# Long convolution of the latents: the exchange between the inverse block transform and the last transform goes through DRAM

## The chip, the cores and the metric

The kernel runs on one core of a Trainium2 chip, in one launch. The metric is the device time of that core in microseconds (us). The kernel before took 2639.78 us, the median of 3 runs (2636.53 to 2640.61).

## What is computed

One inference step of a hybrid block serves 1024 latent tokens and 256 context tokens of width 1024: a SwiGLU, a mixer and a second SwiGLU, with modulated norms between them. Half of the mixer's channels (512) go through a state-space scan, the other half through two long convolutions in a row. Only the long convolution of the latents is touched:

```python
k2 = jnp.concatenate([k[:, 0], jnp.zeros_like(k[:1, 0]), k[:0:-1, 1]], axis=0)
kf = jnp.fft.rfft(k2, axis=0)
zz = v
for i, gate in enumerate((x1, x2)):
    sf = jnp.fft.rfft(zz, n=2 * l, axis=1)
    conv = jnp.fft.irfft(sf * kf[:, i], n=2 * l, axis=1)[:, :l]
    zz = gate * (conv + zz * skip[i])
```

Here l is 1024, so each convolution is a transform of length 2048 per channel, a product with the filter's spectrum, and the transform back.

## The kernel before, in words

The kernel has stages in time: the filters, the first SwiGLU, the projections with the scan, then the long convolutions (`hyena_lat` for the latents, `hyena_ctx` for the context), the output projection (`wout`) and the second SwiGLU. Everything but the long convolutions and a few small parts stays as it is. In the profile the long convolutions lie between 1448 and 1650 us.

A transform of length 2048 is done as matrix products in two steps, 32 = 16 pairs by 64. The 512 channels are worked on in two halves of 256 (`hf` 0 and 1, called left and right here), and there are two convolutions in a row (`o` 0 and 1). For each `o` and `hf` there are three kinds of items:

- **a**, 4 items: transposes of the signal (`pz`), its split in two parts, the first matrix product (`pa`), and a copy to the tile `uu`.
- **b**, 8 items, each two of the 16 blocks: four transposes of `uu` (`pt`, L1403), a copy (`ut`, L1409), the product with the block's matrix (`pzz`, L1414), the product with the filter's spectrum on VectorE and ScalarE (`yy`, L1419 to L1423), the inverse block transform (`pw`, L1431) and a copy by ScalarE to the tile `vv` (L1435). The spectrum is read from DRAM by four DMAs of 128 KB (`ka` L1394, `kb` L1398) into tiles of a ring with three places, two of which each item takes.
- **c**, 8 items, each a pair `w` of 16 rows: four transposes of `vv` (`pt`, L1457), a copy by ScalarE (`vt`, L1463), and the last transform (`py`, L1469) that sums over all 16 blocks. After each four c items come skip and gate on VectorE (`tm`, L1479, L1482), and for the second convolution a split to `yp`, which the output projection reads.

A c item needs all eight b items of its half, since it reads some of each block: this is the exchange. In `pw` the spectrum tile is the stationary operand, so channels come out as partitions and rows as columns; the transposes of `vv` turn a (row, block) slice back to partitions. All matmuls of `pw`, `pzz` and `py` are float32, and each shows as two instructions in the trace; a transpose shows as one.

What sets the order: `weave` writes one list of items out of three streams (left, right, context), taking at each position the ready item with the lowest rank. An item is ready when the items that it names lie a given number of positions back (b after a: 4, c after b: 8, the next a after c: 4). `pipe` then emits the steps of an item one position apart (`s0` at its own position, the next step at the next). A framework fixes each engine's queue at build time, by this order among what it reckons ready, and adds the waits. Each engine works through its own queue in order. All DMAs are issued by SyncE (SP in the profile). By `weave`, the order of items is: b left of the first convolution alone; c left with b right, one of each in turn; c right with b left of the second convolution; c left with b right of the second convolution; and at the end c right alone. The context's items (`pzr`, `pzi`, `pyc`) and the a items lie between them.

Of the kernel before, what the change touches and what calls it, by code (L numbers as in the profile page):

```python
# [110 lines left out]
class Kern:  # L111
# [1225 lines left out]
    def hyena_lat(self, hc, tp, yh, pp, ptag):  # L1337
# [3 lines left out]
        for q in range(4):  # L1341
            nc.sync.dma_start(z[q], self.hyd[q][:, :LAT])
        cb, cbi, cai = ld("cb", [128, 16, 128]), ld("cbi", [128, 16, 128]), ld("cai", [128, 2, 128])
        ca = [hc.tile([128, 256], F32R, name=f"ca{n}") for n in "hl"]
# [40 lines left out]
        def stage_b(o, hf, b2):  # L1385
            r = {}

            def s0():
                if b2 == 0:
                    st["v", hf] = tp.tile([128, 2, 64, 32], F32, name="vv", tag=f"v{hf}", bufs=1)  # L1390
                r["ka"], r["kb"] = t2("ka", "k", 3), t2("kb", "k", 3)
                k = self.kd[o, b2, :, hf]
# [33 lines left out]
            def s5():  # L1426
                r["pw"] = pst("pw")
                pwv = r["pw"].rearrange("p (q n b s) -> p q n b s", q=2, b=2, s=2)
                for q in range(2):
                    for bb in range(2):  # L1430
                        nc.tensor.matmul(pwv[:, q, :, bb, :], r["y"][:, bb, 128 * q:128 * q + 128],  # L1431
                                         cbi[:, 2 * b2 + bb, :], start=True, stop=True)

            def s6():
                nc.scalar.copy(st["v", hf][:, :, :, 4 * b2:4 * b2 + 4],  # L1435
                               r["pw"].rearrange("p (q n s) -> p q n s", q=2, s=4))
            return [s0, s1, s2, s3, None, None, s5, s6]

        def stage_c(o, hf, v2, v):
# [3 lines left out]
            def s0():  # L1443
                if v == 0:
                    st["py", hf] = [pst("py"), pst("py")]
                if v == 0 and v2 == 0:
                    st["g", hf] = []
                    for q in qs:
                        g = self.raw(f"gate{q}")
                        nc.sync.dma_start(g, self.hyd[4 + 4 * o + q][:, :LAT])  # L1450
                        st["g", hf].append(g)
                r["pys"] = st["py", hf]
                r["pt"] = pst("pt2")
                for ww in range(2):
                    for q in range(2):
                        w = 8 * v2 + 2 * v + ww
                        nc.tensor.transpose(out=r["pt"][:, 256 * ww + 128 * q:256 * ww + 128 * q + 128],  # L1457
                                            in_=st["v", hf][:, q, 4 * w:4 * w + 4, :].rearrange("p n s -> p (n s)"),
                                            identity=self.ident)

            def s1():
                r["vt"] = t2("vt", "ut", 2)
                nc.scalar.copy(r["vt"], pv(r["pt"]))  # L1463

            def s2():
# [6 lines left out]
            def s3():  # L1472
                for q in range(2):
# [9 lines left out]
                    if o:  # L1483
                        for gg in range(2):
                            sg = lambda t: t.rearrange("p (n m) -> p n m", m=64)[:, :, 32 * v2:32 * v2 + 32]
                            self.split(tm[:, 8 * gg:8 * gg + 8, :], *[sg(yh[n][gg][qq][:, 0:512]) for n in range(2)])
            return [s0, s1, s2] + ([s3] if v == 3 else [])

        streams = []
        for hf in range(2):  # L1490
            q = []
            for o in range(2):
                p = o - 1
                need = {"a": [(("c", p, hf, 7), 4)] if o else [], "b": [(("a", o, hf, 3), 4)], "c": [(("b", o, hf, 7), 8)]}
                for kind, its in (("a", [stage_a(o, hf, i2) for i2 in range(4)]),
# [414 lines left out]
def _consts():  # L1910
# [66 lines left out]
    for w in range(2):  # L1977
        for m in range(4):
            for b in range(16):
# [3 lines left out]
                else:  # L1983
                    ai[w, m, b, 0, :, 4 * w + m] = 2 * np.cos(tau * b * r / 32)
                    ai[w, m, b, 1, :, 4 * w + m] = -2 * np.sin(tau * b * r / 32)
    out["cai"] = (ai / 2048).reshape(2, 128, 128).transpose(1, 0, 2)
    tt, f = np.arange(256), np.arange(256)
# [88 lines left out]
```

## Time and profile before

| | us |
|---|---|
| median of 3 runs | 2639.78 |
| the profiled execution, its own time | 2639.89 |
| its span | 2638.1 |
| TensorE (PE) busy in the span | 2552.9 (97%) |
| VectorE (DVE) busy | 1610.3 (61%) |
| ScalarE (ACT) busy | 1061.0 (40%) |
| stretch of the long convolutions, 1448 to 1650 | 202 |
| PE busy in that stretch | 185.18 |
| DVE and ACT busy in that stretch | 123.08 and 142.66 |

The span is the time from the first instruction to the last of one profiled execution. PE is busy nearly all the time over the whole kernel; in the stretch of the long convolutions it is less so. Busy time counts an instruction from its start to its modelled end, and the instructions of PE overlap: the next one starts before the one before has ended.

### The profile page before, as it was taken

What the parts mean: (1) busy time and instruction counts of PE and PEld (TensorE: products, weight loads), DVE (VectorE), ACT (ScalarE), POOL (GpSimd) and SP (SyncE); (2) the same over time, 40 slices, a digit from 0 to 9 for tenths busy, and PEclk for the clock granted to TensorE, in tenths of its full rate; (3) what the DMA queues carried; (4) which work ended last, traced back from release to release, by engine and by line L of the source; (5) the groups of instructions that cost most, each with busy time, mean ns of one, the idle gap of its engine ahead of it and who ended that gap; (6) DMA issues with size and microseconds to landing.
All of it is one profiled execution on the core that took longest, in us unless ns stands there. A gap on an engine that the chain in (4) does not pass through costs nothing.

```text
span 2638.1 us, 39050 instructions
## 1 busy us (share of the span) xinstructions
PE 2552.9 (97%) x15373; PEld 2296.1 (87%) x15373; DVE 1610.3 (61%) x2700; ACT 1061.0 (40%) x1832; POOL 2.4 (0%) x7
## 2 busy tenths in 40 slices
PE   7889999999999999999999899998999999999998
PEld 3559999999988788897778788997999999988888
DVE  7879888865467457507884566578454554443445
ACT  5673222222233335415773686354222222232233
POOL 0000000000000000000000000000000000000000
PEclk9989999999999999999999999998999999999999
DMA  7423444332286446211224453731222222263434
GB/s 262 144 88 103 127 141 132 127 102 73 66 279 216 144 155 197 73 49 57 73 75 164 128 153 115 231 114 49 85 62 69 79 64 67 79 210 117 137 121 152
DMA packets 159180, 321.66 MB, mean 122 GB/s; under 512 B 18055, under 2 KB 62991, under 8 KB 158611
## 3 DMA queue, kind: packets, MB, share of 16 engines
q1 hardware_dynamic: 158995, 319.15, 37.6%
q8 instruction: 121, 1.98, 0.3%
q14 instruction: 64, 0.52, 0.1%
HBM read 250.26 MB, written 68.82 MB: 121 GB/s over the span
## 4 chain that ended last, share of the span: by engine, by line
PE 85%; DVE 6%; ACT 4%; DMA 3%; issue 2%; SPq 0%; DVEq 0%; ACTq 0%
PE pp L653 13%; PE pp L652 13%; PE pp L654 13%; PE pd L653 7%; PE pd L652 7%; PE pd L654 7%; PE pc L652 3%; PE pc L654 3%; PE pc L653 3%; PE po L653 1%; PE po L654 1%; PE po L652 1%; PE pseg L991 1%; DMA wd<-wdn 1%; PE pfa L1239 1%
## 5 line engine op out<-in xcount | busy, mean ns | idle before, releaser
L653 PE MATMUL pd<-hs,dh 128*128 128x512 f32 (+1 forms) x1008 | 358.2, 356 | 0.2
L652 PE MATMUL pd<-hs,dh 128*128 128x512 f32 (+1 forms) x1008 | 355.9, 356 | 2.0 <-DVE nm L226 1.6
L654 PE MATMUL pd<-hs,dl 128*128 128x512 f32 (+1 forms) x1008 | 357.4, 356 | 0.1
L139 DVE TENSOR_TENSOR dl<-wd,dh 128x1024 fp32r<-128x1024 f32 x106 | 129.6, 1224 | 196.0 <-ACT dh L138 190.3
L138 ACT CAST wT<-t 128x512 fp32r<-128x512 f32 x168 | 103.8, 620 | 320.4 <-PE pp L654 234.9
L138 ACT CAST dh<-wd 128x1024 fp32r<-128x1024 f32 x106 | 111.1, 1048 | 298.6 <-PE pd L653 191.7
L652 PEld LDWEIGHTS pd<-hs,dh 128*128 128x128 f32 x1008 | 188.7, 188 | 34.2 <-DVE nm L226 3.8
L652 PE MATMUL pp<-yp,wT 128*128 128x320 f32 x672 | 210.4, 313 | 7.3 <-ACT yp L138 3.8
L653 PEld LDWEIGHTS pd<-hs,dh 128*128 128x128 f32 x1008 | 190.1, 189 | 29.2 <-DVE hs L139 0.6
L654 PEld LDWEIGHTS pd<-hs,dl 128*128 128x128 f32 x1008 | 189.8, 188 | 28.8 <-DVE dl L139 0.5
L652 PE MATMUL pp<-sy,wT 128*128 128x320 f32 x672 | 208.9, 311 | 3.1 <-ACT sy L138 3.1
L654 PE MATMUL pp<-yp,wT 128*128 128x320 f32 x672 | 209.7, 312 | 0.0
L654 PE MATMUL pp<-sy,wT 128*128 128x320 f32 x672 | 208.3, 310 | 0.0
L652 PE MATMUL pp<-sh,wB 128*128 128x320 f32 x672 | 208.0, 309 | 0.0
L654 PE MATMUL pp<-sh,wB 128*128 128x320 f32 x672 | 207.5, 309 | 0.0
L179 DVE CUSTOM_DVE_ANT_0 junk<-wa,scb 128x1024 bf16<-128x1024 f32 x144 | 175.7, 1220 | 41.0 <-DMA wa<-wada 39.9
L139 DVE TENSOR_TENSOR wT<-t,wT 128x512 fp32r<-128x512 f32 x168 | 115.4, 687 | 74.4 <-ACT wT L138 74.0
L138 ACT CAST wB<-wg 128x512 fp32r<-128x512 f32 x126 | 78.0, 621 | 203.4 <-PE pp L654 132.3
L652 PE MATMUL pc<-h,wh 128*128 128x512 f32 (+1 forms) x432 | 156.3, 362 | 0.5 <-DVE xr L615 0.5
L653 PE MATMUL pc<-h,wh 128*128 128x512 f32 (+1 forms) x432 | 154.2, 357 | 0.0
L654 PE MATMUL pc<-h,wl 128*128 128x512 f32 (+1 forms) x432 | 154.1, 357 | 0.0
L652 PEld LDWEIGHTS pp<-yp,wT 128*128 128x128 f32 x672 | 128.2, 191 | 8.2 <-ACT yp L138 4.5
(391 smaller groups left out, 6207.1 us busy)
## 6 DMA issues: line engine op xcount, KB each, us to landing
wd<-wdn SPq DMA_DIRECT2D x100, 512.0 KB, 3.7
wg<-wgu SPq DMA_DIRECT2D x84, 512.0 KB, 3.8
wa<-wada SPq DMA_DIRECT2D x72, 512.0 KB, 3.8
hraw<-hida SPq DMA_DIRECT2D x42, 256.0 KB, 3.6
hraw<-hidd SPq DMA_DIRECT2D x42, 256.0 KB, 3.1
wr<-wc SPq DMA_DIRECT2D x18, 512.0 KB, 3.5
kd<-fk SPq DMA_DIRECT2D x32, 256.0 KB, 2.5
ka<-kd SPq DMA_DIRECT2D x64, 128.0 KB, 2.7
```

Of the source, the lines that this page charges most:

```text
L138: nc.scalar.copy(hi, src)
L139: nc.vector.tensor_tensor(out=lo, in0=src, in1=hi.bitcast(F32), op=ALU.subtract)
L179: nc.vector.tensor_tensor_reduce(out=junk, in0=w, in1=self.scb[cond], scale=1.0, scalar=0.0, op0=ALU.mult, op1=ALU.add, accum_out=self.mod ...
L652: nc.tensor.matmul(ps, wh, rh, start=first, stop=False, **more)
L653: nc.tensor.matmul(ps, wh, rl, start=False, stop=False, **more)
L654: nc.tensor.matmul(ps, wl, rh, start=False, stop=last, **more)
L991: nc.tensor.matmul(q["seg"], self.trir[:, d, :], t, start=d == 0 and n == 0, stop=d == 1 and n == 1)
L1239: nc.tensor.matmul(r["pa"][:, qs], r["k2"][:, qs], caf, start=True, stop=True)
```

## The change

The inverse block transform `pw` gets its operands exchanged: the block's matrix `cbi` is the stationary operand and the product `yy` the moving one, so rows come out as partitions and the 256 channels as columns. Two products of 256 columns take the place of four of 128. ScalarE copies the result to a new tile `vw` (ring of three), and two DMAs per b item write it to a DRAM tile `zv`. A c item reads its pair of rows from `zv` by one DMA straight into `vt` (ring of four), with (block, row) as partitions; its transposes and its ScalarE copy are gone, and the last product `py` stays with a reordered constant. The tile `vv` is gone, the ring of `ka` and `kb` has six places in place of three, and `py` of a c item is emitted three positions after its first step (it was two). The next a items may follow five positions after the last c (it was four).

```diff
@@ stage_b
             def s0():
-                if b2 == 0:
-                    st["v", hf] = tp.tile([128, 2, 64, 32], F32, name="vv", tag=f"v{hf}", bufs=1)
-                r["ka"], r["kb"] = t2("ka", "k", 3), t2("kb", "k", 3)
+                r["ka"], r["kb"] = t2("ka", "k", 6), t2("kb", "k", 6)
...
             def s5():
                 r["pw"] = pst("pw")
-                pwv = r["pw"].rearrange("p (q n b s) -> p q n b s", q=2, b=2, s=2)
-                for q in range(2):
-                    for bb in range(2):
-                        nc.tensor.matmul(pwv[:, q, :, bb, :], r["y"][:, bb, 128 * q:128 * q + 128],
-                                         cbi[:, 2 * b2 + bb, :], start=True, stop=True)
+                for bb in range(2):
+                    nc.tensor.matmul(r["pw"][:, 256 * bb:256 * bb + 256], cbi[:, 2 * b2 + bb, :], r["y"][:, bb, :],
+                                     start=True, stop=True)
 
             def s6():
-                nc.scalar.copy(st["v", hf][:, :, :, 4 * b2:4 * b2 + 4],
-                               r["pw"].rearrange("p (q n s) -> p q n s", q=2, s=4))
+                t = t2("vw", "vw", 3)
+                nc.scalar.copy(t, pv(r["pw"]))
+                for bb in range(2):
+                    nc.sync.dma_start(self.zv[o][hf][:, 2 * b2 + bb], t[:, bb, :])
...
@@ stage_c
-                r["pt"] = pst("pt2")
-                for ww in range(2):
-                    for q in range(2):
-                        w = 8 * v2 + 2 * v + ww
-                        nc.tensor.transpose(out=r["pt"][:, 256 * ww + 128 * q:256 * ww + 128 * q + 128],
-                                            in_=st["v", hf][:, q, 4 * w:4 * w + 4, :].rearrange("p n s -> p (n s)"),
-                                            identity=self.ident)
-
-            def s1():
-                r["vt"] = t2("vt", "ut", 2)
-                nc.scalar.copy(r["vt"], pv(r["pt"]))
-
+                r["vt"] = t2("vt", "vt", 4)
+                w = 8 * v2 + 2 * v
+                nc.sync.dma_start(r["vt"], self.zv[o][hf][w:w + 2].rearrange("w b r c -> (b r) w c"))
...
-            return [s0, s1, s2] + ([s3] if v == 3 else [])
-
+            return [s0, None, None, s2] + ([s3] if v == 3 else [])
+
+        self.zv = [[self.dp.tile([16, 16, 8, 256], F32, name=f"zv{o}{hf}") for hf in range(2)] for o in range(2)]
...
-                need = {"a": [(("c", p, hf, 7), 4)] if o else [], "b": [(("a", o, hf, 3), 4)], "c": [(("b", o, hf, 7), 8)]}
+                need = {"a": [(("c", p, hf, 7), 5)] if o else [], "b": [(("a", o, hf, 3), 4)], "c": [(("b", o, hf, 7), 8)]}
```

The constant `cai` is stored with its 128 rows in the new order (`caih`).

## Rows read from the trace of the kernel before

**Rows 1.** Chain that ended last between 1440 and 1665 us, shares by line.

```profile
by line: PE py L1469 8.4%; PE pw L1431 7.9%; ACT uu L1381 7.0%; PE pzz L1414 5.5%; issue 5.3%; PE pt L1457 4.0%; DVE yy L1422 3.4%; PE pzr L1538 3.3%; DMA yraw<-ysd 3.2%; ACT yy L1421 3.1%; PE pyc L1561 3.1%; PE pzi L1538 3.1%; ACT yy L1420
```

**Rows 2.** Stretches: us; PE, PEld, DVE, ACT, POOL busy (count); clock, DMA share, GB/s.

```profile
1463.60:1503.50 39.90, 35.52 (x203) 28.84 (x202) 25.27 (x39) 27.12 (x42) 0.00 (x0) 0.96 0.48 146
...
1618.00:1634.60 16.60, 13.17 (x72) 11.70 (x70) 13.01 (x29) 8.49 (x21) 0.00 (x0) 0.90 0.54 175
1634.60:1650.00 15.40, 14.31 (x98) 13.85 (x99) 6.71 (x13) 9.52 (x18) 0.00 (x0) 0.77 0.21 69
```

**Rows 3.** TensorE in order of time: one pair of b and c items, 1520 to 1525.

```profile
1521.06 1.06 PE L1469 MATMUL py<-c_cai,vt 128*128 128x128 f32 x8
1521.95 0.60 PE L1457 MATMUL pt<-ident,vv 128*128 128x128 f32 x4
1522.39 1.06 PE L1431 MATMUL pw<-c_cbi,yy 128*128 128x128 f32 x8
1523.29 1.03 PE L1414 MATMUL pzz<-ut,c_cb 128*128 128x256 f32 x4
1524.15 0.60 PE L1403 MATMUL pt<-ident,uu 128*128 128x128 f32 x4
```

**Rows 4.** Groups of instructions, 1446 to 1655: busy us, mean ns, idle before.

```profile
L1457 PE MATMUL pt<-ident,vv 128*128 128x128 f32 x128 | 20.0, 287 | 0.7 <-ACT vv L1435 0.7
...
L1435 ACT COPY vv<-pw 128x512 f32<-128x512 f32 x32 | 18.7, 589 | 8.6 <-PE pw L1431 8.3
```

**Rows 5.** Issues on the spectrum's DRAM tensor: ns min/median/max on the SP queue.

```profile
L1394 SPq DMA_DIRECT2D ka<-kd x64: 444/448/1465, 1451.9 to 1622.9; - x64
L1398 SPq DMA_DIRECT2D kb<-kd x64: 444/588/607, 1453.0 to 1624.6; - x64
L1277 SPq DMA_DIRECT2D kd<-fk x32: 512/513/1010, 92.2 to 185.3; - x32
```

**Rows 6.** DMA issues of 140 to 190 and of 1446 to 1655: us to landing.

```profile
kd<-fk SPq DMA_DIRECT2D x16, 256.0 KB, 2.4
...
gatec<-hyd SPq DMA_DIRECT2D x4, 256.0 KB, 2.8
```

**Rows 7.** The last of `pw` and the first of c: first convolution left, right, second left.

```profile
1497.73 1.05 PE L1431 MATMUL pw<-c_cbi,yy 128*128 128x128 f32 x8
...
1503.51 1.04 PE L1457 MATMUL pt<-ident,vv 128*128 128x128 f32 x8
...
1542.71 1.05 PE L1431 MATMUL pw<-c_cbi,yy 128*128 128x128 f32 x8
...
1545.47 1.04 PE L1457 MATMUL pt<-ident,vv 128*128 128x128 f32 x8
...
1582.14 1.13 PE L1431 MATMUL pw<-c_cbi,yy 128*128 128x128 f32 x8 [1.25 <-DVE yy L1423]
...
1592.83 1.04 PE L1457 MATMUL pt<-ident,vv 128*128 128x128 f32 x8
```

**Rows 8.** What the SP queue waited for, 1400 to 1680: us, times, longest.

```profile
SPq L1398 <- DVE yy L1419: 31.1, 10, 7.4
```

**Rows 9.** Chain of waits, then instructions in time: last b, last c items.

```profile
1622.92 5.08 DMA ka<-kd
...
1632.48 2.05 PE L1431 MATMUL pw<-c_cbi,yy 128*128 128x128 f32 x8 [3.36 <-DVE yy L1423]
1637.05 2.08 PE L1469 MATMUL py<-c_cai,vt 128*128 128x128 f32 x8
1638.92 1.06 PE L1457 MATMUL pt<-ident,vv 128*128 128x128 f32 x4
1648.83 1.16 PE L1469 MATMUL py<-c_cai,vt 128*128 128x128 f32 x8 [0.48 <-ACT vt L1463]
```

**Rows 10.** A stretch of the mixed stage, and SP issues beside other large transfers.

```profile
1552.00:1572.00 20.00, 19.57 (x153) 18.39 (x153) 14.37 (x24) 16.03 (x29) 0.00 (x0) 1.00 0.47 140
...
92.25 3.13 SPq L1277 DMA_DIRECT2D kd<-fk  x3
```

More of the change, by code (lines that the diff above doesn't have):

```diff
@@ L1342, in hyena_lat @@
             nc.sync.dma_start(z[q], self.hyd[q][:, :LAT])
-        cb, cbi, cai = ld("cb", [128, 16, 128]), ld("cbi", [128, 16, 128]), ld("cai", [128, 2, 128])
+        cb, cbi, cai = ld("cb", [128, 16, 128]), ld("cbi", [128, 16, 128]), ld("caih", [128, 2, 128])
         ca = [hc.tile([128, 256], F32R, name=f"ca{n}") for n in "hl"]
@@ L1985, in _consts @@
                     ai[w, m, b, 1, :, 4 * w + m] = -2 * np.sin(tau * b * r / 32)
-    out["cai"] = (ai / 2048).reshape(2, 128, 128).transpose(1, 0, 2)
+    out["caih"] = (ai / 2048).reshape(2, 4, 16, 2, 128).transpose(2, 1, 3, 0, 4).reshape(128, 2, 128)
     tt, f = np.arange(256), np.arange(256)
```

## The prediction

> **What bounds the kernel now.** I began with the page's busy shares and its slices: TensorE is near full all along and thins out only a little between 1448 and 1650 us, where the long convolutions lie. So the question is whether TensorE sets the end in that stretch too. The chain of waits answers it [rows 1]: TensorE's lines lead (`py`, `pw`, `pzz`), but ScalarE's copies, VectorE's `yy` and issue have shares of several per cent, so it is a mixture. The table by stretch splits the mixture [rows 2, 10]. In the mixed stages, where c items of one half alternate with b items of the other, TensorE is busy 19.57 of 20 us: it is the bound there. In 1463.6 to 1503.5, mostly b items alone, it is busy 35.52 of 39.9; at the end, 1618 to 1634.6, 13.17 of 16.6, and the clock falls (0.90, then 0.77).
>
> What TensorE needs for a pair of items is read from starts in order of time [rows 3]: `py` 1521.06 to 1521.95, 0.89; transposes of `vv` 0.44; `pw` 0.90; `pzz` 0.86; transposes of `uu` another 0.44 (the same four instructions). That is 3.53 us per pair.
>
> The Trainium skill ("Trainium Kernel Development and Optimization", Performance Expectations) says matmul busy time is a poor measure because matmuls are pipelined. The row agrees: the 32 groups of `vv` transposes have 20.0 us busy [rows 4], 0.63 each, against 0.44 by their starts. By busy time the first term below would be 24 x 0.63 = 15.1 instead of 10.6, and the forecast 4.5 us lower.
>
> **The change part by part.**
>
> *Transposes of `vv` and their copy.* 24 of the 32 c items lie in three mixed stages that TensorE bounds; each loses 0.44: 24 x 0.44 = 10.6 us gained. The ScalarE copies that go (32, of the form that took 0.589 [rows 4]) gain nothing by themselves, as ScalarE has slack there (16.03 of 20 [rows 10]); bounds 0 to 2 us, I take 0.
>
> *`pw` with exchanged operands.* Four instructions of 256 columns, as `pzz` has: 0.86 for 0.90 [rows 3]. 24 x 0.04 = 1.0 us gained. Its copy has the same shape.
>
> *Three more DMA issues per pair on the SP queue.* Nearest row for both write and read: an issue of 256 KB in 1 KB rows, 0.513 [rows 5]. Loads cost 2 x 0.448 + 2 x 0.588 = 2.07 per b item, so a pair needs 2.07 + 3 x 0.513 = 3.61 us of SP, more than the 3.05 us that TensorE would then need (3.53 - 0.44 - 0.04). What hides it is the ring of six: loads of three items can go out before a mixed stage begins. Inside a stage of eight pairs there are then five loads, about five pairs of writes (a write comes seven positions after its item's load) and eight reads: 5 x 2.07 + 5 x 1.03 + 8 x 0.51 = 19.6 of 24.4 us. I take 0. Without that cover the pair goes at 3.61 and the 11.6 us of the first two terms become a loss of 24 x 0.08 = 1.9. The writes wait for ScalarE's copy; behind them in the queue stand reads and later loads, which are used three positions after their issue at the earliest.
>
> *DMA engines.* Loads alone take a share of 0.47 at 140 GB/s [rows 10], so 298 GB/s would fill them. A stage's loads (5 x 0.524 MB), writes (5 x 0.262) and reads (8 x 0.262) are 6.0 MB or 20.2 us of 24.4: 83%. It fits, with little room; cost 0 to 3 us, I take 0.
>
> *Round trip at the start of c.* The first `py` now waits for copy 0.59 [rows 4], two write issues 1.03 [rows 5], a landing 2.4 and a read's landing 2.8 [rows 6]: 6.8 us after the last `pw`. Before it was copy, transposes, copy: 1.6 without waits. Left, first convolution: last `pw` ends about 1498.6 (start and 0.90), other work runs to 1503.5 [rows 7], cover 4.9, so a gap of 1.9; now it is 0.15, since the eight transposes fill 0.88 of the 1.03 until the first copy is done: +1.75. Right: `pw` ends about 1543.6, cover to 1545.5, a gap of up to 4.9 against 0.15, but b items of the other half are nearly ready and can be put into it: between 0 and 4.75, I take 1.55. Left, second convolution: from 1583.0 to 1592.8 other products run [rows 7], 9.8 of cover: 0. Together +3.3 (0 to 6.5).
>
> *The ring of six, b items alone.* The SP queue waited 31.1 us for `kb` places in ten waits [rows 8]. TensorE's idle time in that stretch is 4.4 us [rows 2]; the gain lies between 0 and that. VectorE's chain through `yy` (three places, unchanged) is late next, so I take 2.
>
> *The ring of six, last b item.* Its `ka` was issued at 1622.92 and took 5.08 to land; `pw` followed at 1632.48 after 3.36 idle, and at a clock that had fallen took 2.05 instead of 1.06 [rows 9, 3]. Loaded three items earlier, the item waits for nothing but its `pzz`, and its VectorE and ScalarE steps lie beside the products that TensorE still has. Gain 0 to 4.4, I take 4.
>
> *The last eight c items alone.* Nothing covers the round trip here. Before: from the copy to the end of `py` about 1634.6 to 1650, 15.4 us [rows 2, 9]. After: 6.8 for the round trip; TensorE idles meanwhile, and after an idle time half as long the clock fell to 1.2 GHz for some us (mean 0.77 [rows 2], `py` 1.87 apart, 1637.05 to 1638.92 [rows 9]). Three `py` at 1.87 and five at 0.89 make 10.1. 16.9 against 15.4: +1.5. Bounds: no fall of the clock and a faster trip, -2; reads that come in two rounds through the ring of four, or stand behind weight loads of the output projection in the SP queue, +6.
>
> Sum: -10.6 - 1.0 + 3.3 - 2 - 4 + 1.5 = -12.8. From the profiled execution's 2639.9 (span 2638.1 and 1.8 around it), which is the median of the runs to 0.1: **2627**.
>
> **Rivals.**
>
> 1. *The SP queue sets the pace, no change.* The loads are not taken ahead in time and a pair takes 3.61. For: 3.61 is well above 3.05, and a load can go out early only if its place is free and nothing that waits stands ahead of it. Against: six places hold the loads of three items. +1.9 + 3.3 - 2 - 4 + 1.5 = +0.7: 2641, or a little below where some loads come early.
>
> 2. *The queue is stopped by its own writes, slower.* A pair of writes at the head of the SP queue waits for ScalarE's copy, and loads behind it are late for VectorE, which makes the next copy late. With one copy's 0.59 per pair: 3.61 + 0.59 = 4.20, 24 x 0.67 = +16.1, with the other terms (-1.2) +14.9: 2655. It is slower by over 0.2% from 3.80 per pair on, a stop of 0.19. For: three issues beside other transfers took 3.13 us [rows 10], so a full DMA system alone can stretch issues that far. Against: loads have three positions of slack.
>
> 3. *Landings are late.* The trip's landings come out near the longest here, 5.08 [rows 9] in place of 2.4 for the writes: 2.7 more at three starts (the fourth is covered), +8: 2635. For: DMA engines at 83%. Against: 2.4 and 2.8 are medians of quiet and of busy stretches. The Trainium skill ("Perfetto Trace Analysis", DMA Instruction — HWDGE) says the write's completion can be surprisingly long when the target is HBM. The rows disagree so far: DRAM writes land in 2.4, reads in 2.8 [rows 6].
>
> That the exchange isn't replaced as described (transposes remain) can be excluded: nothing else transposes in c.
>
> **How the numbers follow.** Forecast 0.54, with its own range 2617 to 2634 (bounds about the sum: the trip +3.2 and -3.3, the two ring terms +6 and -2.8, the end +4.5 and -3.5, not all at once). Rival 1 0.20, rival 2 0.14, rival 3 0.12. 0.2% is 5.3 us, about what a measurement of this kernel can tell from no change. Rival 3 lies at that line and is halved: faster 0.60. Rival 1 and the other half: same 0.25. Slower 0.15. The range for 8 in 10 takes in the forecast, rivals 1 and 3: 2616 to 2645; rival 2 is left out.
>
> **What would show it.** In the mixed stages `py` of neighbouring c items should start 3.05 to 3.2 apart in place of 3.53; 3.6 speaks for rival 1, 3.8 and more, with SP waiting on ScalarE's copy, for rival 2. VectorE should wait no more for `ka` before the last `yy`. Before the last eight `py` TensorE should be idle for about 6 us and its clock lower after it. The landings of `zv` writes and `vt` reads should be 2.4 and 2.8. The forecast is wrong if the mixed stages don't shrink by some 3.5 us each, or if gaps at the starts of c exceed 3 us.

## The result, and the profile after

The changed kernel takes **2655.36 us**, the median of 4 runs (2651.58 to 2657.58), against 2640.2 for the kernel before: a ratio of 1.006, with an interval of 1.0048 to 1.0072. It is slower by 0.6%; the forecast was 2627. The profiled span is 2655.7 against 2638.1, so 17.6 us came on top, 17.1 of them between the first `pz` and the last `py`. Line numbers are the changed kernel's from here on: `pzz` L1412, `yy` L1417 to L1421, `pw` L1427, its copy L1432, the write L1434, the read L1453, `py` L1458.

The same stretches in both kernels, cut where items begin. Columns: stretch and its length in us, then busy us (count) of TensorE, its weight loads, VectorE, ScalarE, GpSimd, granted clock, share of the DMA engines, GB/s. First the kernel before, its three mixed stages (first `py` of a half to last `pw` of the next) and its end:

```profile
1504.78:1542.71 37.93, 36.99 (x276) 34.66 (x277) 24.29 (x38) 29.21 (x48) 0.00 (x0) 1.00 0.45 140
1547.55:1582.14 34.59, 32.80 (x252) 30.66 (x253) 22.10 (x35) 26.25 (x45) 0.00 (x0) 1.00 0.50 145
1594.11:1632.48 38.37, 34.05 (x240) 31.55 (x241) 29.18 (x54) 25.31 (x50) 0.00 (x0) 0.99 0.43 137
1632.48:1649.99 17.51, 16.34 (x106) 15.59 (x107) 8.29 (x18) 10.05 (x20) 0.00 (x0) 0.74 0.19 63
```

Then the changed kernel; its first row is the stretch of b items alone [rows 2]:

```profile
1473.90:1501.63 27.73, 23.95 (x106) 17.87 (x105) 19.87 (x31) 18.87 (x31) 0.00 (x0) 0.94 0.64 190
1509.64:1545.69 36.05, 33.72 (x213) 29.90 (x213) 23.53 (x39) 20.94 (x36) 0.00 (x0) 1.00 0.74 215
1555.18:1595.42 40.24, 37.12 (x193) 29.80 (x194) 24.89 (x39) 18.76 (x34) 0.00 (x0) 0.94 0.71 210
1607.11:1644.95 37.84, 29.61 (x174) 25.13 (x173) 26.57 (x50) 23.31 (x47) 0.00 (x0) 0.96 0.68 198
1644.95:1667.50 22.55, 12.76 (x70) 11.55 (x71) 8.61 (x17) 5.51 (x11) 0.00 (x0) 0.61 0.68 211
```

Read the lengths against the counts. TensorE has some sixty fewer instructions in each mixed stage, yet the three last 36.05, 40.24 and 37.84 us instead of 37.93, 34.59 and 38.37. By the forecast they should have lost some 3.5 each. The sign that the forecast named, `py` of neighbouring c items 3.05 to 3.2 us apart, can't be read: single distances lie between 0.9 and 6.5 us, their means in the three stages are 2.76, 3.92 and 3.34, and before they were 2.83, 3.09 and 2.86. The end grew from 17.51 to 22.55 with TensorE busy only 12.76 of it, and the clock fell further, to a mean of 0.61.

The pair in order of time [rows 3]; columns: start, us, engine, line, operation, tiles, shapes, in brackets the idle time before and what ended it:

```profile
1560.74 1.05 PE L1458 MATMUL py<-c_caih,vt 128*128 128x128 f32 x8
...
1564.80 1.10 PE L1427 MATMUL pw<-yy,c_cbi 128*128 128x256 f32 x4 [0.76 <-DVE yy L1421]
...
1567.91 1.13 PE L1427 MATMUL pw<-yy,c_cbi 128*128 128x256 f32 x4 [0.71 <-DVE yy L1421]
1568.88 1.05 PE L1458 MATMUL py<-c_caih,vt 128*128 128x128 f32 x8
1569.77 1.03 PE L1412 MATMUL pzz<-ut,c_cb 128*128 128x256 f32 x4
1570.64 0.60 PE L1401 MATMUL pt<-ident,uu 128*128 128x128 f32 x4
1571.07 1.08 PE L1458 MATMUL py<-c_caih,vt 128*128 128x128 f32 x8
1572.94 1.10 PE L1427 MATMUL pw<-yy,c_cbi 128*128 128x256 f32 x4 [0.78 <-DVE yy L1421]
```

By starts, `py` is 0.89 (1568.88 to 1569.77), `pzz` 0.87 and the transposes 0.43, as before, and `pw` 0.97 (1567.91 to 1568.88). But before each of the three `pw` shown TensorE stands idle for 0.7 to 0.8 us until VectorE's sum L1421 is done.

The SP queue in the same place, back to back (start, us from the first of the merged issues to the end of the last, queue, line, tiles, number of issues):

```profile
1566.57 1.19 SPq L1434 DMA_DIRECT2D zv<-vw  x2
1567.85 0.55 SPq L1453 DMA_DIRECT2D vt<-zv  x1
1568.49 1.11 SPq L1392 DMA_DIRECT2D ka<-kd  x2
1569.69 1.19 SPq L1396 DMA_DIRECT2D kb<-kd  x2
1570.97 1.19 SPq L1434 DMA_DIRECT2D zv<-vw  x2
1572.26 0.54 SPq L1453 DMA_DIRECT2D vt<-zv  x1
1572.89 1.11 SPq L1392 DMA_DIRECT2D ka<-kd  x2
1574.09 2.17 SPq L1396 DMA_DIRECT2D kb<-kd  x2
1576.36 1.19 SPq L1434 DMA_DIRECT2D zv<-vw  x2
```

A pair takes 4.40 us of the queue (1566.57 to 1570.97), the next 5.39. The forecast had 3.61: one issue of a `ka` load has a median of 0.584 us now [rows 5 had 0.448], while the median landings came out as forecast [rows 6]; the longest read took 6.1 us. The queue was full in this stretch, but not throughout: over the three mixed stages it waited 11.3, 9.9 and 13.7 us, 35 of 114. Three answers for the whole stretch of the long convolutions: the issues of L1392 (ns min/median/max), landings (median us), the two longest waits of the queue (us, times, longest; before [rows 8]):

```profile
L1392 SPq DMA_DIRECT2D ka<-kd x64: 444/584/1198, 1452.3 to 1632.5; - x64
```

```profile
zv<-vw SPq DMA_DIRECT2D x64, 128.0 KB, 2.4
vt<-zv SPq DMA_DIRECT2D x32, 256.0 KB, 2.9
```

```profile
SPq L1434 <- ACT vw L1432: 14.2, 14, 2.1
SPq L1392 <- DVE yy L1417: 11.3, 4, 8.0
```

The end [rows 9], first the SP queue, then TensorE:

```profile
1647.65 1.17 SPq L1434 DMA_DIRECT2D zv<-vw  x2
1648.91 1.04 SPq L154 DMA_DIRECT2D wr<-wo  x2
1650.82 1.91 SPq L1453 DMA_DIRECT2D vt<-zv  x4
1655.87 0.34 SPq L154 DMA_DIRECT2D wr<-wo  x1
1658.68 5.14 SPq L1453 DMA_DIRECT2D vt<-zv  x4
```

```profile
1644.95 2.04 PE L1427 MATMUL pw<-yy,c_cbi 128*128 128x256 f32 x4 [0.95 <-DVE yy L1421]
1656.60 8.44 PE L1458 MATMUL py<-c_caih,vt 128*128 128x128 f32 x48 [9.60 <-DMA vt<-zv]
1665.22 2.29 PE L1458 MATMUL py<-c_caih,vt 128*128 128x128 f32 x16 [0.18 <-DMA vt<-zv]
```

Two weight loads of 512 KB went out at 1648.91 ahead of the four reads. From the copy of the last `pw` to the first `py` TensorE stood still for 9.60 us; the forecast had 6.8 for this way. The clock had fallen before that: 0.71 was granted from 1640 to 1645, with TensorE busy for 2.03 of the 5 us, and 0.50, the lower of its two levels (1.2 GHz), from 1645 to 1660, so that the last `pw` took 2.04 us where those above took 1.10. The last reads went out in a second round, from 1658.68.

Last, a place that the forecast did not look at: the entry, from the first signal transposes (`pz`) to the first `pw`, where the transposed signal is split (the waits of ScalarE and VectorE there: us in total, times, longest):

```profile
DVE ztl L139 <- DMA hyd<-hyt: 2.7, 1, 2.7
ACT zth L138 <- DMA hyd<-hyt: 0.6, 1, 0.6
```

Nothing of this stands in the trace of before. `hyd<-hyt` is a store of the stage ahead.

### The profile page after: what moved, and what is told of

It is laid out like the page before. It is cut to its first block, busy times and chain, and to the rows that moved or that the text cites. A ratio compares the mean times of both kernels' runs of the same rounds, so it can differ in the third digit from the quotient of the medians.

```text
span 2655.7 us, 38644 instructions
## 1 busy us (share of the span) xinstructions
PE 2548.1 (96%) x15117; PEld 2284.6 (86%) x15117; DVE 1609.2 (61%) x2700; ACT 1042.7 (39%) x1800; POOL 2.4 (0%) x7
## 5 line engine op out<-in xcount | busy, mean ns | idle before, releaser
L139 DVE TENSOR_TENSOR dl<-wd,dh 128x1024 fp32r<-128x1024 f32 x106 | 129.4, 1223 | 193.9 <-ACT dh L138 188.2
L654 PEld LDWEIGHTS pd<-hs,dl 128*128 128x128 f32 x1008 | 189.7, 188 | 27.9
```

Of the source, the lines that this page charges most:

```text
L139: nc.vector.tensor_tensor(out=lo, in0=src, in1=hi.bitcast(F32), op=ALU.subtract)
L654: nc.tensor.matmul(ps, wl, rh, start=False, stop=last, **more)
```

## The experiments

All stretches by the starts of items in the traces, in us; "start" is the time from the last `pw` of a half to its first `py`.

| stretch | before | after | e5 | e6 | e7 | e9 | e4 |
|---|---|---|---|---|---|---|---|
| entry: first `pz` to first `pw` | 21.8 | 25.4 | 21.8 | 21.8 | 21.8 | 21.8 | 21.7 |
| b alone (8 items) and left start | 34.9 | 35.7 | 35.7 | 31.3 | 29.8 | 27.7 | 34.2 |
| mixed 1 and right start | 42.8 | 45.5 | 45.9 | 44.1 | 45.3 | 42.6 | 39.3 |
| mixed 2 and left start | 46.6 | 51.9 | 49.5 | 50.0 | 48.1 | 44.6 | 44.8 |
| mixed 3 | 38.4 | 37.9 | 37.9 | 34.7 | 35.6 | 35.3 | 37.2 |
| end: last `pw` to last `py` | 17.5 | 22.6 | 22.4 | 20.6 | 19.5 | 9.9 | 10.8 |
| all | 201.9 | 219.0 | 213.2 | 202.4 | 200.0 | 181.8 | 188.2 |
| time | 2639.8 | 2655.4 | 2652.5 | 2640.3 | 2640.0 | 2623.1 | 2629.0 |

A stage and the start behind it stand together, since the changed order moves a and context items from one to the other. The stretches of a column are those of one execution; the time is the median of the runs. How far a stretch can be read shows from e5: it differs from the changed kernel by a longer ring of `vw`, for whose places ScalarE had never waited, and yet its second mixed stage with the start is 2.4 us shorter. So single differences of that size show little; those that repeat over several kernels are used. The columns e4 to e9 are experiments, told below.

**Is it the SP queue or the bytes?** (A and B in the expectations.)

> The changed kernel with each write to the DRAM tile and each read of it cut to half of the channels (128 of 256), as many DMA issues as before; the other half of the last transform's input is wrong, and the products keep their number. Theory A, the SP queue's issues set the pace of the mixed stages (about 4.4 us per pair of b and c items: seven issues of 0.5 to 0.6 us and the gaps between them): bytes don't matter, pairs stay at 4.2 to 4.5 us, total 2650 to 2656 us. Theory B, the 16 DMA engines are full (share 0.65 to 0.8 in these stages): 8 MB less traffic, pairs fall to 3.6 us or below, total near 2640 us or less.

```diff
-nc.sync.dma_start(self.zv[o][hf][:, 2 * b2 + bb], t[:, bb, :])
+nc.sync.dma_start(self.zv[o][hf][:, 2 * b2 + bb, :, 0:128], t[:, bb, 0:128])
```

(the read likewise.) 2649.19 us, ratio 1.0034 (1.0023 to 1.0045).

> The changed kernel with the DRAM tile laid out so that one DMA per b item writes both blocks (256 KB in rows of 2 KB) in place of two; same bytes, six issues per pair in place of seven. Theory A (SP issues): 0.6 us less per pair, 3.8 us, 24 x 0.6 = 14 us in the mixed stages if SP stays the bound and some of it at the three starts of c, total 2638 to 2646 us. Theory B (DMA bytes): 2652 to 2656 us.

```diff
-for bb in range(2):
-    nc.sync.dma_start(self.zv[o][hf][:, 2 * b2 + bb], t[:, bb, :])
+nc.sync.dma_start(self.zv[o][hf].rearrange("w r b c -> (w r) b c")[:, 2 * b2:2 * b2 + 2], t)
```

2650.5 us, 1.004 (1.0025 to 1.0055).

> The changed kernel with the two writes per b item issued by ScalarE's own queue, behind its copy, in place of SP. Theory A (SP issues): SP needs 3.2 us per pair, so pairs fall to 3.1 to 3.5 us unless ScalarE, which now holds two issues per b item (about 1.2 us), becomes the bound; total 2632 to 2645 us. Theory B (DMA bytes): 2652 to 2656 us.

```diff
-    nc.sync.dma_start(self.zv[o][hf][:, 2 * b2 + bb], t[:, bb, :])
+    nc.scalar.dma_start(self.zv[o][hf][:, 2 * b2 + bb], t[:, bb, :])
```

2655.6 us, 1.006 (1.0045 to 1.0075): no change, though SP lost two of its seven issues per pair and never waited for the copy. Neither theory has this pattern: fewer bytes and fewer issues were each worth 5 to 6 us (the interval of e2 touches that of the changed kernel), less than A or B said, and moving the writes nothing. Rival 2 of the forecast, writes that stop the SP queue, gets no support from e3; the result met its price (2655) by chance. e3 doesn't refute it alone, since the issues only moved: each took 0.54 us (median) on ScalarE's queue, 1.1 us per b item, beside the copies that a b item needs. By stretch its first two mixed stages with their starts are 48.9 and 52.2 us, longer than the 45.5 and 51.9 of the changed kernel, the third and the end 36.6 and 19.4, shorter. The Trainium skill ("DMA: Bandwidth & Descriptors", Issuing engines are not separate DMA queues) says that the issuing engines feed the same 16 DMA engines, so that issuing from several engines saves only the time that the issuing takes. The time of e3 is in line with that: 2655.6 us against 2655.4.

**What were the transposes worth?**

> The kernel before without the transposes of vv and their ScalarE copy: the last product reads slices of vv as they are (values wrong), so nothing takes the exchange's place. It measures what the first term of the prediction could bring at most. If TensorE bounds the mixed stages: 24 x 0.44 = 10.6 us there, 3.5 at the end and one or two at the starts, total 2622 to 2629 us, pairs at 3.1 us. If other chains bound them: 2634 to 2640 us.

```diff
-    (c item: four transposes of vv, copy to vt)
-    nc.tensor.matmul(dst, r["vt"][:, ww, 128 * q:128 * q + 128], cai[:, ww, :], ...)
+    nc.tensor.matmul(dst, st["v", hf][:, q, 4 * w:4 * w + 4, :].rearrange("p n s -> p (n s)"), cai[:, ww, :], ...)
```

This is the kernel before, with `py` taking `vv` as it lies. 2629.0 us, 0.9958 (0.9943 to 0.9973). The time is at the edge of what TensorE as the bound would give, but much of it came from elsewhere: the end gave 6.7 us, the mixed stages alone 1.4, 0.5 and 1.2 (from starts of items). With the starts behind them, as in the table, it is 3.5, 1.7 and 1.2, 6.4 in all: the first pair of rows gave the full 8 x 0.44 that TensorE as the bound would give, the second half of it, the third a third. In the stages themselves the reason is seen in the spacing of the `pw` of the eight b items: 4.06, 3.77 and 4.12 us on average before, 4.00, 3.74 and 4.05 without transposes. The c items ran ahead (`py` 1.67 apart in the first stage, 2.83 before); the b items kept their pace. The three mixed stages of e4, to be set against the first three rows of before above:

```profile
1504.46:1541.00 36.54, 34.53 (x253) 32.20 (x252) 25.17 (x40) 25.29 (x41) 0.00 (x0) 1.00 0.49 145
1543.77:1577.86 34.09, 30.93 (x230) 28.31 (x229) 22.27 (x35) 24.57 (x42) 0.00 (x0) 1.00 0.54 155
1588.59:1625.82 37.23, 31.95 (x218) 29.09 (x216) 30.91 (x58) 21.68 (x45) 0.00 (x0) 1.00 0.50 149
```

TensorE's idle time grew from 0.9, 1.8 and 4.3 us to 2.0, 3.2 and 5.3, and its waits for VectorE's sum before a `pw` from 0.8, 0.4 and none to 2.0, 2.3 and 5.3: part of what was taken off came back as gaps.

**The entry.**

> The changed kernel with nothing else than a ring of nine buffers instead of three for vw, so that the pool of the stage is as large as in the kernel before (90 KB instead of 78 KB) and the tiles behind it lie where they lay before. Theory placement: the 3.6 us that the changed kernel loses between the first pz transpose and the first pw (25.38 us against 21.75 before) are a wait of the splits into zth and ztl on the older DMAs hyd<-hyt, which still read the memory that the smaller pool now takes. Then this stretch falls back to 21.7 to 22.2 us, all later stretches stay, and the time is 2651 to 2653 us. Rival: the longer entry comes from the work of the stage itself (the longer queue of loads, ring of six): then the stretch stays at 25 to 25.6 us and the time at 2655.

```diff
-t = t2("vw", "vw", 3)
+t = t2("vw", "vw", 9)
```

The entry is back at 21.76 us and the time at 2652.46 (1.0047, 1.0034 to 1.0061), 2.9 us less than the changed kernel. The wait for `hyd<-hyt` is gone from its trace. So 3.6 us of the stretch's loss had nothing to do with the way of the exchange: without `vv` and with other rings the stage's pool shrank from 90 to 78 KB, its tiles came to lie on memory that the stage ahead was still storing from, and the first splits waited for that store.

**The ring of `yy`.**

> The changed kernel with one write for each b item instead of two (as in e2_one_write), a ring of five instead of three for yy and yy2, and vw at seven so that the pool is 90 KB. Theory of the element-wise chain: where b items run alone they start 3.33 us apart or more because yy and yy2 wait for buffers (three of them, two taken by each item), and with the loads' ring of six nothing else is late; then pw0 to pw7 falls from 27.7 us to 22 to 25 us, the mixed stages by 1 to 2 us each, and the time is 2635 to 2643 us. Rival one: VectorE's and ScalarE's own work is the bound in these stretches, and the ring changes nothing: pw0 to pw7 stays at 27.5 to 28.3 us and the time is that of e2_one_write less the 3.6 us of the entry, 2646 to 2648 us. Rival two: SP's queue is the bound: pw0 to pw7 falls (4 issues for an item there), the mixed stages do not, 2640 to 2645 us.

```diff
-y, y2 = t2("yy", "yy", 3), t2("yy2", "yy", 3)
+y, y2 = t2("yy", "yy", 5), t2("yy2", "yy", 5)   # and e2's single write, vw at 7
```

2640.3 us, 1.0001 (0.9992 to 1.001). The eight b items alone went from 28.2 us (e2) to 23.2, as the theory of the chain had it. Of the mixed stages only the third fell (37.7 to 34.7; the others 34.4 to 35.4 and 38.1 to 38.1), so in those two the ring is not what holds the pace. The stretch of b items alone, to be set against 27.73 above:

```profile
1468.77:1491.97 23.20, 21.96 (x106) 16.36 (x105) 17.98 (x29) 18.12 (x30) 0.00 (x0) 1.00 0.68 210
```

The same on the kernel before:

> The kernel before, with four buffers instead of three for yy and yy2 and one instead of two for tm (the same pool of 90 KB). Theory: the kernel before, too, is held by the ring of yy: its eight b items alone start 3.33 us apart because the second of two items finds no buffer, and in the mixed stages the same chain of a b item stands right behind TensorE; with room for two whole items pw0 to pw7 falls from 27.85 us to 23 to 25.5 us and the mixed stages by up to 1 us each: 2631 to 2636 us. Then the gain of e6_yy_ring_five over e2_one_write beyond the entry is the ring's and nothing of the exchange. Rival: only five buffers (a whole item in each of two steps and one to spare) or the ring of loads of three stands in its way: 27 to 28 us for pw0 to pw7, 2638 to 2641 us.

```diff
-y, y2 = t2("yy", "yy", 3), t2("yy2", "yy", 3)
+y, y2 = t2("yy", "yy", 4), t2("yy2", "yy", 4)   # and tm with one buffer
```

b items alone 24.9 us instead of 27.9, the end 4.2 shorter; 2638.05 us, 0.999 (0.998 to 1.0). The ring is a fault of the kernel before as well and owes nothing to the exchange. The stage gained 7.5 us and what follows it lost 4.9.

> The kernel before with four buffers for yy, as e12_before_yy_four, but the last product of the second convolution is written into z, which is dead then, and the splits into yp and ys read it there; so the one buffer of tm is free as soon as VectorE has read it. In e12_before_yy_four the stage was 7.5 us shorter (201.9 to 194.4) and what follows 4.9 us longer (988.1 to 993.0): there VectorE's tm of each next quarter waited for ScalarE's split of the last one. Theory: with that wait gone what follows falls back to 988 to 990 us and the time is 2631 to 2634 us. Rival: the time given back is the next stage's weights (wr<-wo), which are no earlier: 2636 to 2639 us.

```diff
-nc.vector.tensor_tensor(out=zz if o == 0 else tm, in0=tm, in1=sl(st["g", hf][q]), op=ALU.mult)
+nc.vector.tensor_tensor(out=zz, in0=tm, in1=sl(st["g", hf][q]), op=ALU.mult)
```

2638.39 us, 0.9997 (0.9989 to 1.0006): the stage is 5.2 us shorter than before, what follows 2.4 longer (990.5 against 988.1), and the time is not measurably better. The rival holds: a shorter end is partly given back to the weights and splits of the output projection.

**Relieving the queue.**

> e6_yy_ring_five, and the loads of ka and kb fetch two b items at once: four DMAs of twice the size for two items instead of eight, from a kd whose items lie in fours; the ring holds four tiles of twice the size (the bytes loaded are the same). SP then issues in a mixed pair 2 loads, 1 write and 1 read, some 2.3 us instead of the 4.4 to 5.4 us that were seen. Theory SP's queue: the mixed stages fall to the TensorE chain's or the element-wise chain's pace, 3.05 to 3.4 us for a pair, py8 to py15e 22 to 23.5 us; 2630 to 2638 us. Rival, DMA bytes: a pair moves as many bytes as before, the stages stay as in e6_yy_ring_five within 1 us each, and the time within 2 us of it.

```diff
-r["ka"], r["kb"] = t2("ka", "k", 6), t2("kb", "k", 6)   # four loads of 128 KB for each b item
+if b2 % 2 == 0:                                          # four loads of 256 KB for two b items
+    t = st[n, hf] = tp.tile([128, 4, 256], F32, name=n, tag="k", bufs=4)
```

2639.99 us (0.9999, 0.999 to 1.0008), within 0.3 of e6, as the rival had it. SP's issues for a pair fell from six to four (seven in the changed kernel), and the rows of the three mixed stages changed by 1.2, -1.9 and 0.9 us, 0.2 in all; so a full SP queue, the forecast's rival 1, was not what set their end. The DMA engines were now 80% busy (the first mixed stage):

```profile
1500.10:1536.24 36.14, 33.09 (x212) 29.88 (x213) 25.32 (x43) 21.99 (x37) 0.00 (x0) 1.00 0.80 219
```

On top of e7, first the edit of e1, then that of e3:

> e7_loads_in_pairs with half the columns written and read in the exchange (128 of 256; the py products of both q take the same half; the other half of the values is left out), as many DMAs as there. Theory DMA bytes: with SP's queue relieved, the DMA engines (80% busy, 220 GB/s in the first mixed stage) set the time at which vt, ka and kb land (6.3, 3.4 and 5.4 us there); a quarter fewer bytes bring the three mixed stages and the starts down by 1.5 to 3 us each: 2628 to 2635 us. Rival, SP's queue stands behind the copies whatever the bytes are: stages within 1 us of e7_loads_in_pairs, the time within 3 us of 2640.

```diff
-nc.sync.dma_start(self.zv[o][hf]...[:, 2 * b2:2 * b2 + 2], t)
+nc.sync.dma_start(self.zv[o][hf]...[:, 2 * b2:2 * b2 + 2, 0:128], t[:, :, 0:128])
```

> e7_loads_in_pairs with the exchange's writes issued from ScalarE's queue, right behind the copy to vw, instead of SP's. Theory SP's queue stands behind the copies: in the first mixed stage of e7_loads_in_pairs SP waits 19.2 of 36 us for the copy to vw, and the reads and loads behind the write wait with it; with the write elsewhere the mixed stages fall by 2 to 4 us each: 2628 to 2634 us. Rival, DMA bytes: the reads and loads go out earlier but land as late: 2637 to 2643 us. Rival, order: no change either.

```diff
-nc.sync.dma_start(self.zv[o][hf]..., t)
+nc.scalar.dma_start(self.zv[o][hf]..., t)
```

Half the bytes: 2637.25 us (0.9985, 0.9975 to 0.9994), 2.7 less than e7. That is less than the bytes theory wanted (5 to 12 us) and within the 3 us of its rival, and the intervals of e7 and e10 touch, so that bytes were worth little, if anything. The writes on ScalarE's queue: 2642.36 (1.0006, 0.9996 to 1.0017), nothing.

**No exchange at all.**

> e7_loads_in_pairs without the exchange: pw is still copied to vw, but nothing is written to or read from DRAM, and the py products take a constant (cb) as their stationary operand in place of vt; the c items still come after the b items that they came after. It leaves out the passing on of the values. So TensorE has no transposes of the exchange, yy has five buffers, SP issues loads only. Theory wait for the exchange: what holds the mixed stages of e7_loads_in_pairs at 36.1, 37.7 and 35.6 us is the way of the values through DRAM (copy, write, read, 6.3 us median to land in the first of them, DMA engines 80% busy) and the queue of SP, which stood 19 of 36 us behind the copies to vw. Then they fall to 29 to 33 us each and the time to 2600 to 2618 us. Rival, order of the work: the in-order queues of VectorE and ScalarE and the interleaving of the streams set the pace, and it makes little difference where the values come from: stages of 34 to 37 us; with the short starts and the short end that e4_no_transposes had, 2618 to 2630 us.

```diff
-nc.sync.dma_start(self.zv[o][hf]..., t)          # the write
-nc.sync.dma_start(r["vt"], self.zv[o][hf]...)    # the read
-nc.tensor.matmul(dst, r["vt"][:, ww, 128 * q:128 * q + 128], cai[:, ww, :], ...)
+nc.tensor.matmul(dst, cb[:, 2 * ww + q, :], cai[:, ww, :], ...)
```

2623.1 us (0.9925, 0.991 to 0.994). Its mixed stages and its end:

```profile
1496.30:1531.09 34.79, 32.62 (x214) 29.74 (x212) 25.44 (x43) 21.63 (x37) 0.00 (x0) 1.00 0.57 156
1538.85:1574.20 35.35, 33.93 (x194) 27.48 (x193) 27.11 (x43) 19.99 (x34) 0.00 (x0) 1.00 0.58 156
1583.44:1618.77 35.33, 28.60 (x174) 24.74 (x173) 27.73 (x54) 23.59 (x49) 0.00 (x0) 1.00 0.40 112
1618.77:1628.66 9.89, 9.89 (x68) 9.46 (x68) 4.04 (x10) 2.85 (x6) 0.00 (x0) 0.83 0.19 55
```

This is the central run. No transposes, nothing through DRAM, five places for `yy`, a quiet SP queue, and the mixed stages still take 34.8 to 35.4 us: the theory of the wait said 29 to 33, the rival, order of the work, 34 to 37. The `pw` of the b items are 3.77, 4.03 and 3.69 apart, in e7 3.82, 4.12 and 3.75. Set against e7, the way through DRAM costs 16.9 us in time (19.5 by each one's ratio to the kernel before); by the table 9.6 of 18.2 at the end, 8.4 in the three rows that hold a start of c, 0.3 in the third mixed stage. One reading is not excluded: in the first two of these stages TensorE is busy 94 and 96%, so there its own work may be what is left as the bound. The second holds 16 of the context's `pzr` and `pzi` products, which in the kernel before lay behind it, so equal lengths against before say little. In the third, with 81%, it hardly can.

> e9_no_exchange (the exchange's values left out) with the last of the three VectorE operations of a b item, the sum of y and y2, on GpSimd, which is idle in the stage; VectorE has 0.69 us less for each b item, 5.5 us of a mixed stage. Theory VectorE's throughput: in e9_no_exchange VectorE was busy 30.1, 30.2 and 31.0 of the 34.8, 35.4 and 35.3 us of the mixed stages, and that is what replaced TensorE; then they fall by 3 to 5 us each and the time to 2608 to 2615 us. Theory chain: a b item goes pt, ut, pzz, the copies on ScalarE, three steps on VectorE and pw through three engines that each work in order, and each mixed stage lasts as long as some eight passes of it; a sum on GpSimd, surely not faster than VectorE's 0.69 us, lengthens each pass: the mixed stages stay or grow by up to 8 us each, and the time is 2622 to 2645 us.

```diff
-nc.vector.tensor_tensor(out=y, in0=y, in1=y2, op=ALU.add)
+nc.gpsimd.tensor_tensor(out=y, in0=y, in1=y2, op=ALU.add)
```

2634.22 us (0.9979, 0.997 to 0.9988), 11.1 more than e9, in the range of the chain theory:

```profile
1497.35:1539.00 41.65, 36.17 (x214) 32.49 (x212) 23.53 (x35) 22.50 (x38) 10.48 (x8) 0.92 0.49 135
1545.92:1583.33 37.41, 34.32 (x194) 27.43 (x193) 21.86 (x34) 20.02 (x35) 10.47 (x8) 1.00 0.50 142
1593.27:1631.35 38.08, 28.68 (x174) 24.70 (x173) 25.55 (x46) 23.70 (x49) 11.12 (x8) 0.98 0.36 106
```

VectorE is less busy (23.53, 21.86, 25.55 us against 25.44, 27.11, 27.73) and every stage is longer. (The expectation's 30 to 31 us for e9 were sums of durations that overlap.) So VectorE's throughput is not the bound; a longer step in a b item's chain makes the stage longer. By how much: the sum takes 0.64 us more on GpSimd, and the product before it (L1421) 0.11 more beside it (last section), which is 6.0 us for eight items. With their starts the first stage grew by 6.0, the second and the third by 2.8 each, and in the first the granted clock fell to 0.92 as well. So the chain is not all of the pace in the later two.

**The ring of six, and the last half by transposes.**

> The changed kernel with the loads' ring back at three (ka and kb share it), in the pool of 90 KB of e5_pool_90k (vw at twelve); to be compared with e5_pool_90k, 2652.5 us. The forecast gave the ring of six 6 us: 4 at the last b item (stretch from the last py of the third stage to the last pw, 13.4 us in e5_pool_90k, then 17 again) and 2 where b items run alone. By the forecast: 2657 to 2660 us. By the ring of yy (which e6_yy_ring_five showed to set the b items' pace where they run alone): pw0 to pw7 stays at 27.7 us. If the mixed stages are held by SP's queue, the ring of six is worth more in them, since a load that waits for a buffer of the ring holds the exchange's reads behind it: 2660 us and more. Rival: the ring is worth nothing, 2651 to 2654 us.

```diff
-r["ka"], r["kb"] = t2("ka", "k", 6), t2("kb", "k", 6)
+r["ka"], r["kb"] = t2("ka", "k", 3), t2("kb", "k", 3)   # vw at twelve
```

2657.82 us (1.0068, 1.0053 to 1.0084) against 2652.46 of e5: the ring of six is worth 5.4 us, near the 6 forecast, but elsewhere: 3.7 for b alone and the left start, 1.2 and 3.2 for the first two mixed stages with their starts, while the third and the end gave back 2.3. From the last `py` of the third stage to the last `pw` it took 14.9 us (13.4 in e5), not 17. `pw` 0 to `pw` 7 did not stay at 27.7, it was 25.7, with a left start of 13.7 behind it: only the two together can be compared.

> e7_loads_in_pairs, and the right half of the second convolution, whose last eight c items have no b items beside them, goes the old way: its pw is computed with y as the stationary operand, copied into vv, and the c items transpose it on TensorE; the other three halves go through DRAM. Theory: the round trip and the ring of four at the end cost what pw31 to the last py is longer than before (22.6 against 17.5 us); with the old way there it is 16.5 to 18 us, and the time 4 to 6 us under e7_loads_in_pairs. Rival: the end is long because TensorE runs there at its lower clock (0.55 granted between 1640 and 1660 us in the changed kernel), which the old way's 32 transposes meet as well: 20 us or more, and a time within 2.5 us of e7_loads_in_pairs.

```diff
+if o and hf:   # pw with y stationary, its copy to vv, and in c the old transposes and vt copy
+    nc.tensor.matmul(pwv[:, q, :, bb, :], r["y"][:, bb, 128 * q:128 * q + 128], cbi[:, 2 * b2 + bb, :], ...)
```

2639.09 us (0.9995, 0.9986 to 1.0004). The end fell from 19.5 to 16.4, about as expected, but the time only by 0.9: the entry was 1.1 longer and what follows 1.8.

No version that passes on all values is faster than the kernel before by what can be told apart: e12 and e15 without the change, e8 with part of it and e7 with all of it lie between 0.999 and 1.0 of it.

## Why the prediction was wrong, step by step

**"TensorE bounds the mixed stages", 10.6 us: this step failed, and with it the forecast.** The reading was that 19.57 busy us of 20 [rows 10] make TensorE the bound, and that a pair costs the 3.53 us of one close pair [rows 3]. That row is a part of one stage: over the whole stages before, TensorE was idle for 0.9, 1.8 and 4.3 us. And the eight b items of a stage are 3.77 to 4.12 us apart before, and stay within 0.1 us of that when the transposes are free (e4). In e4 the three stages alone gave 3.0 us, with their starts 6.4, not 10.6. The changed kernel's three stages took 114.1 us against 110.9. What is likely is that a b item's own way through in-order engines sets much of the pace: `pt`, copy, `pzz`, two copies on ScalarE, three steps on VectorE, `pw`. Work that is not urgent fills the gaps, so that every engine looks well used; taking work from one opens gaps on it, as e4 shows. e13 supports this, since a longer step in that way made all three stages longer, and shows that it is not VectorE's throughput. Which link of the chain binds in each pass stays open, and so does whether TensorE's own work binds in the first two stages once the exchange is gone (94 and 96% busy in e9).

**`pw` with exchanged operands, 1.0 us:** no gain is seen; it took 0.97 by its starts above against 0.90 before.

**DMA issues at 0, "hidden by the ring of six": the size failed, the zero nearly held.** An issue took 0.55 to 0.6 us, not 0.45 to 0.51, and a pair 4.4 to 5.4 of the queue. The queue was full in places, yet taking three of its seven issues away (e6, e7) moved the first two mixed stages little. DMA bytes were worth 2.7 us (e10), hardly clear of nothing and within the forecast's 0 to 3.

**Round trip at the starts, +3.3 (0 to 6.5):** right in kind. From e7 to e9 the left start and the b items before it gave 2.2 us, mixed 1 and right start 2.7, mixed 2 and left start 3.5: 8.4 together, stages included, where the forecast covered the last entirely. What TensorE itself waited for the first reads in the changed kernel is less: 1.92 us at the left start (forecast a gap of 1.9), 0.50 at the right one (between 0 and 4.9), nothing at the second left one, as forecast. So the waits at the starts were sized about right, and the rest of the 8.4 lies elsewhere in these rows.

**The ring of six, -2 and -4:** 5.4 us in all (e14), right in sum; the b items alone were still held by the ring of `yy`, which the forecast named as next in line (e6: 28.2 to 23.2 us).

**The end, +1.5 (-2 to +6):** +5.05, near the upper bound, and both reasons given with it are seen: weight loads ahead of the reads, and two rounds through the ring of four. From the last copy to the first `py` it took 9.6 us, where the forecast had 6.8; how much each reason adds was not measured. By what is gained when the exchange is left out, the transposes cost 6.7 us at the end before (before against e4), the way through DRAM also 9.6 (e7 against e9).

**Not in the sum at all:** the entry, 3.6 us (e5), from a pool that got smaller.

By stretch, in us, the forecast had -0.3 for b alone and left start, -2.3 and -3.9 for the first two mixed stages with their starts, -7.9 for the third, +1.5 for the end, and 0 for the entry. Measured: +0.8, +2.8, +5.4 (+2.9 in e5), -0.5, +5.1, +3.6, which is 17.1 before rounding. The two ways of exchange can be priced apart, each against a kernel that leaves the exchange out: by TensorE 10.8 us (before against e4), less than its 32 x 0.44 = 14.1 us of TensorE time; by DRAM 16.9 us (e7 against e9) with the best queue that was tried. The two prices stem from kernels with different rings, so their difference, 6.1 us, is rough. With the entry's 3.6 it leaves some 5 of the 15 us that the changed kernel lost, about what the single write of e2, which e7 has too, was worth (4.9).

## What to carry to other kernels

A busy share of 98% in one stretch and one pair of items do not make an engine the bound. Measure the spacing of the slowest kind of item over a whole stage, and ask which chain that item goes through; where the spacing exceeds what the engine needs for all its work in that time, work taken off the engine can return as gaps. A kernel that leaves the work out, run first, says what taking it away is worth. When a tile leaves a pool, look at what the neighbours then lie on: a pool's size is part of the schedule. And price the places without cover, the starts and the end, first: there a transfer's whole way counts.

## What the runs showed of the hardware that was not expected

In e13 GpSimd took 1.33 us for the sum that VectorE does in 0.69, and VectorE's own operations with both operands in SBUF became slower beside it, while those with an operand from PSUM did not (L1418, `ka` times `pzz`, stayed at 683 ns). First e9, then e13 (busy us, mean ns, idle before):

```profile
L1421 DVE TENSOR_TENSOR yy<-kb,yy 128x512 f32<-128x512 f32 x32 | 22.1, 690 | 13.8 <-ACT yy L1420 13.3
...
L1467 DVE TENSOR_TENSOR z<-tm,gate 128x512 f32<-128x512 f32 x8 | 5.5, 685 | 0.0
```

```profile
L1422 POOL TENSOR_TENSOR yy<-yy,yy 128x512 f32<-128x512 f32 x32 | 42.5, 1330 | 1585.7 <-DVE yy L1421 1555.6 <-PE py L1454 16.2 <-PE pzz L1413 10.5
...
L1421 DVE TENSOR_TENSOR yy<-kb,yy 128x512 f32<-128x512 f32 x32 | 25.7, 804 | 23.7 <-ACT yy L1420 22.2 <-issue 1.3
...
L1467 DVE TENSOR_TENSOR z<-tm,gate 128x512 f32<-128x512 f32 x8 | 6.4, 831 | 0.0
```

The Trainium skill ("SBUF — State Buffer", Who interferes with whom) says that a VectorE instruction with two SBUF inputs contends with a GpSimd instruction that reads SBUF, and that one with at most one such input, outside the 2-port performance modes, does not. The rows agree: 690 to 804 ns and 685 to 831 ns for the first kind, no change for the second.
